# A two-layer encoder on one core: lead-in of the first sublayer with raw x transposed, the norm's division behind the products, and weight jobs that serve both token blocks

## The chip, the cores and the metric

One core of one Trainium2 chip. The metric is device microseconds (us) of the whole program, the median of several runs.

## What is computed

Six sublayers in a row over x of 256 tokens by 1024 channels, float32. The change touches the first one only, a half-step feed-forward network:

```python
def _rmsnorm(x, g, eps=RMS_EPS):
    y = xf * lax.rsqrt(jnp.mean(xf * xf, axis=-1, keepdims=True) + eps)
    return y * g

def _half_ffn(x, g_pre, g_post, w_gate, w_up, w_down):      # widths 1024 -> 2816 -> 1024
    h = _rmsnorm(x, g_pre)
    f = (jax.nn.silu(h @ w_gate) * (h @ w_up)) @ w_down
    return x + 0.5 * _rmsnorm(f, g_post)
```

The six are: this network (a), a convolution module (b), the network twice more with other weights (c, d), differential attention (e), the network again (f).

## The kernel before

**Numbers.** Each product of float32 values is made of three products in a rounded format (`mm3`, L151): both operands are split into a high part (`xTh`, `wh`, cast by ScalarE) and a low part (`xTl`, `wl`, the difference, by VectorE), and high by high, high by low and low by high are added up in PSUM.

**Weight stream.** All weights come in jobs of half a megabyte. `issue` (L107) asks SyncE's queue for the transfer into one of 5 `raw` buffers, casts the high part on ScalarE (L113) and subtracts on VectorE (L114). The subtraction ends the use of the `raw` buffer. `pump` (L119) keeps up to 12 split jobs ahead of the oldest one in use. For sublayer a the jobs are: 0 and 1 the gate columns of chunk 0 (256 columns, 4 tiles of 128 rows each), 2 and 3 its up columns, 4 to 7 the same of chunk 1, 8 to 11 of chunk 2, then six jobs of the down weight, and so on.

**Lead-in.** SyncE asks for the first 128 tokens of x, the norm weights copied to all 128 partitions (`gain`, L174, half a megabyte), jobs 0 and 1, and the other 128 tokens. `prenorm` (L181) squares a token block on ScalarE (L186), multiplies it by the norm weights on VectorE (L188), takes the root on GpSimd (L163) and multiplies by it (L192); `turn` (L201) transposes the result on TensorE (L205) and splits it into `xTh` (L208) and `xTl` (L209).

**Sublayer a.** `ffn` (L317) takes its first two chunks with `proj_x` (L244): a token block is the stationary operand, and one bank of PSUM (`pxa`, 2 banks in turn, pool `ps_gu`) receives gate and up columns side by side, 48 products for each token block and chunk, in the order block 0, block 1 of chunk 0, then of chunk 1. ScalarE applies Silu to the gate half (L330), VectorE multiplies (L332), TensorE transposes the two halves (`hta`, L334). The other chunks go through `projs` (L261): the weight is the stationary operand, each bank (`gua`) takes 48 products, ScalarE applies Silu (L342), VectorE multiplies (L344). Products with the down weight (`acca`, 512 columns) run in between and after.

**Order.** Each engine runs its instructions in a fixed order. The framework's planner chooses that order before the run by the order in the program, by priority, and by when it expects operands; `keep_in_program_order` pins an instruction behind all earlier ones of its engine.

Of the kernel before, what the change touches and what calls it, by code (L numbers as in the profile page):

```python
# [14 lines left out]
ALU = mybir.AluOpType  # L15
# [22 lines left out]
WARM = (16, 6, 6)  # L38

# [10 lines left out]
def trunk_kernel(  # L50
# [56 lines left out]
    def issue(i):  # L107
        src, shape = jobs[i]
        raw = rawp.tile([P, *shape], F32, tag="raw", name=f"raw{i}")
        nc.sync.dma_start(raw, src)  # L110
        hi = wp.tile([P, *shape], F32R, tag="wh", name=f"wh{i}")
        lo = wp.tile([P, *shape], F32R, tag="wl", name=f"wl{i}")
        A.copy(hi, raw)  # L113
        V.tensor_tensor(lo, raw, r32(hi), ALU.subtract)  # L114
        ready[i] = (hi, lo)

    issued, oldest, gone = [0], [0], set()

    def pump():  # L119
        while issued[0] < min(oldest[0] + NW, len(jobs)):  # L120
            issue(issued[0])
            issued[0] += 1
# [11 lines left out]
    class Weight:  # L134
        """Some k tiles of a weight, in jobs of half a megabyte; w(k) gives hi and lo of tile k."""
# [30 lines left out]
    def spread(ms, rows, name):  # L166
        """rows[i] = ms[:, i]^-1/2, the same in every partition."""
# [13 lines left out]
    def prenorm(tb, g, name):  # L181
# [11 lines left out]
        pending.append(lambda: turn(tb, xn, name))  # L193

# [33 lines left out]
    def spin(n, name):  # L228
        """n products that nobody reads: an idle tensor engine drops to half its clock."""
# [4 lines left out]
    def proj(w1, w2, f, name):  # L234
        """[w1 tile f | w2 tile f].T @ xT -> one bank [128, 2*S]."""
# [8 lines left out]
    def proj_x(pairs, order, name):  # L244
        """x[tb] @ [w1 | w2] for pairs of weights i, as (tb, i, bank [128 tokens, 2*FC])."""
# [14 lines left out]

    def projs(pairs, name):  # L261
        """(tile number, bank) of each pair of columns."""
# [12 lines left out]
    class Down:  # L275
        """y[tok, D] += s[:, tok].T @ W over k tiles; the tail one token block after the other."""
# [38 lines left out]
    TURN = [(tb, i) for i in range(2) for tb in range(NTB)]  # L315

    def ffn(hp, jb, name):  # L317
# [10 lines left out]
        for tb, i, ps in proj_x([r[:2] for r in jb[:2]], TURN if name == "a" else TWO, name):  # L328
            sg = sp.tile([P, FC], F32, tag="sg", name=f"sx{name}{tb}{i}")
            A.activation(sg, ps[:, :FC], AF.Silu)  # L330
            h = sp.tile([P, FC], F32, tag="hf", name=f"hx{name}{tb}{i}")
            V.tensor_tensor(h, ps[:, FC:], sg, ALU.mult)  # L332
            for f in range(2):
                T.transpose(turned[i][:, f, tb, :], h[:, f * P:(f + 1) * P], ident)  # L334
        for i in range(2):
            hi, lo = tiles(i)
            split_to(hi, lo, turned[i])
            put(i, hi, lo)
        for kt, ps in projs([(c, jb[c][:2]) for c in range(2, len(jb))], name):
            c, f = divmod(kt, 2)  # L340
            sg = sp.tile([P, S], F32, tag="sg", name=f"sg{name}{kt}")
            A.activation(sg, ps[:, 0, :], AF.Silu)  # L342
# [447 lines left out]
```

## Time and profile before

| | |
|---|---|
| median of 3 runs | 1060.96 us (1059.96 to 1061.01) |
| span of the profiled execution, first to last instruction | 1059.0 us |
| TensorE busy | 1023.4 us |
| VectorE, ScalarE, GpSimd busy | 659.6, 553.7, 72.4 us |
| moved from HBM | 175.40 MB, 167 GB/s over the span |
| first product of the first sublayer | 11.42 us after the span's start |
| first product with the down weight | 47.52 us after the span's start |

The profiled execution has a span of 1059.0 us; the timed figure is taken around the whole execution and is 2.0 us above it. In the views, PE is TensorE, PEld its loads of stationary operands, DVE VectorE, ACT ScalarE, POOL GpSimd, SPq SyncE's queue; L113 is line 113. A matmul's duration is modelled with its pipeline, so the time from one start to the next, not the printed duration, is what it costs in a stream.

### The profile page before, as it was taken

To read this page: it belongs to the slowest core of one execution; us is meant where nothing else is said; L and a number is where in the kernel's file an instruction comes from. 1 tells how busy PE (TensorE), PEld (TensorE's weight loads), DVE (VectorE), ACT (ScalarE), POOL (GpSimd) and SP (SyncE) were. 2 spreads that over 40 slices of the span, in tenths; PEclk is the share of its full clock that TensorE was granted. 3 is DMA by queue.
4 is the path that set the end of the run, shared out by engine and by line. 5 is a ranking of instruction groups with operands and counts; after the bars stand their busy time and mean duration, and the time that the engine had idled before them with its cause. 6 is when DMAs were issued, how large, how long until landed. Compare 5 with 4: busy or idle time off the path is not lost.

```text
span 1059.0 us, 17905 instructions
## 1 busy us (share of the span) xinstructions
PE 1023.4 (97%) x7133; PEld 947.7 (89%) x7133; DVE 659.6 (62%) x1007; ACT 553.7 (52%) x933; POOL 72.4 (7%) x110
## 2 busy tenths in 40 slices
PE   6999999999969999999999999999999999999997
PEld 5899999899967989999989999998899789999995
DVE  6655556679996755455575555566777685555542
ACT  6564445476845644444455445454577665445431
POOL 1000000031560100000010000001000110000000
PEclk9999999999998999999999999999999999999999
DMA  9877465376000666475555665554842255665511
GB/s 296 283 208 221 150 205 179 112 259 197 14 1 0 215 203 218 148 229 177 165 175 185 195 218 151 190 188 133 276 150 91 80 165 180 196 216 155 187 58 40
DMA packets 130492, 177.62 MB, mean 168 GB/s; under 512 B 6173, under 2 KB 112709, under 8 KB 130408
## 3 DMA queue, kind: packets, MB, share of 16 engines
q1 hardware_dynamic: 130408, 176.47, 52.1%
q8 instruction: 56, 0.92, 0.3%
q14 instruction: 28, 0.23, 0.1%
HBM read 175.40 MB, written 1.05 MB: 167 GB/s over the span
## 4 chain that ended last, share of the span: by engine, by line
PE 79%; DVE 10%; issue 3%; ACT 2%; DMA 2%; POOL 2%; SPq 0%; DVEq 0%; POOLq 0%; ACTq 0%
DVE co L474 4%; PE gud L152 3%; PE gua L152 3%; PE gua L154 3%; PE gud L154 3%; PE gud L153 3%; PE gua L153 3%; PE guc L152 3%; PE guf L152 3%; PE guf L154 3%; PE guc L154 3%; PE guc L153 3%; PE guf L153 3%; DVE wl L114 2%; PE accf L152 2%
## 5 line engine op out<-in xcount | busy, mean ns | idle before, releaser
L114 DVE TENSOR_TENSOR wl<-raw,wh 128x1024 fp32r<-128x1024 f32 x320 | 389.7, 1224 | 135.6 <-ACT wh L113 132.8
L113 ACT CAST wh<-raw 128x1024 fp32r<-128x1024 f32 x320 | 333.9, 1051 | 137.0 <-PE accd L154 14.0
L152 PE MATMUL guc<-xTh,wh 128*128 128x256 f32 x288 | 82.1, 285 | 0.0
L152 PE MATMUL guf<-xTh,wh 128*128 128x256 f32 x288 | 82.0, 285 | 0.0
L152 PE MATMUL gud<-xTh,wh 128*128 128x256 f32 x288 | 82.0, 285 | 0.0
L152 PE MATMUL gua<-xTh,wh 128*128 128x256 f32 x288 | 82.0, 285 | 0.0
L154 PE MATMUL guc<-xTh,wl 128*128 128x256 f32 x288 | 81.7, 284 | 0.0
L154 PE MATMUL gua<-xTh,wl 128*128 128x256 f32 x288 | 81.7, 284 | 0.0
L154 PE MATMUL guf<-xTh,wl 128*128 128x256 f32 x288 | 81.7, 284 | 0.0
L154 PE MATMUL gud<-xTh,wl 128*128 128x256 f32 x288 | 81.7, 284 | 0.0
L153 PE MATMUL gua<-xTl,wh 128*128 128x256 f32 x288 | 81.0, 281 | 0.0
L153 PE MATMUL guc<-xTl,wh 128*128 128x256 f32 x288 | 81.0, 281 | 0.0
L153 PE MATMUL guf<-xTl,wh 128*128 128x256 f32 x288 | 80.9, 281 | 0.0
L153 PE MATMUL gud<-xTl,wh 128*128 128x256 f32 x288 | 80.9, 281 | 0.0
L474 DVE SCALAR_TENSOR_TENSOR co<-u,wdw,co 128x256 f32<-128x256 f32 x120 | 61.9, 581 | 0.0
L153 PEld LDWEIGHTS guc<-xTl,wh 128*128 128x128 f32 x288 | 54.7, 190 | 0.5
L153 PEld LDWEIGHTS gua<-xTl,wh 128*128 128x128 f32 x288 | 54.6, 190 | 0.5
L153 PEld LDWEIGHTS guf<-xTl,wh 128*128 128x128 f32 x288 | 54.6, 190 | 0.5
L153 PEld LDWEIGHTS gud<-xTl,wh 128*128 128x128 f32 x288 | 54.6, 190 | 0.5
L152 PEld LDWEIGHTS guc<-xTh,wh 128*128 128x128 f32 x288 | 54.4, 189 | 0.5
L152 PEld LDWEIGHTS gud<-xTh,wh 128*128 128x128 f32 x288 | 54.4, 189 | 0.5
L152 PEld LDWEIGHTS guf<-xTh,wh 128*128 128x128 f32 x288 | 54.4, 189 | 0.5
(357 smaller groups left out, 2672.4 us busy)
## 6 DMA issues: line engine op xcount, KB each, us to landing
raw<-in_ffn_w_gate_dram SPq DMA_DIRECT2D x88, 512.0 KB, 5.1
raw<-in_ffn_w_up_dram SPq DMA_DIRECT2D x88, 512.0 KB, 4.9
raw<-in_ffn_w_down_dram SPq DMA_DIRECT2D x88, 512.0 KB, 4.8
raw<-in_conv_w_pw_dram SPq DMA_DIRECT2D x24, 512.0 KB, 4.5
raw<-in_attn_w_qkv_dram SPq DMA_DIRECT2D x24, 512.0 KB, 4.7
raw<-in_attn_w_o_dram SPq DMA_DIRECT2D x8, 512.0 KB, 4.9
gpre<-in_ffn_norm_pre_dram SPq DMA_DIRECT2D x3, 512.0 KB
x<-in_x_dram SPq DMA_DIRECT2D x2, 512.0 KB
```

The lines of the kernel that those rows point to most:

```text
L113: A.copy(hi, raw)
L114: V.tensor_tensor(lo, raw, r32(hi), ALU.subtract)
L152: T.matmul(o, sh, mh, start=first, stop=False)
L153: T.matmul(o, sh, ml, start=False, stop=False)
L154: T.matmul(o, sl, mh, start=False, stop=last)
L474: tap[ct, t] = V.scalar_tensor_tensor(c, u[:, t:t + S], wdw[:, ct, t:t + 1], c, ALU.mult, ALU.add)
```

## The change

- The first norm is replaced by `first_norm`, with its order on TensorE, ScalarE, VectorE and SyncE pinned by hand. TensorE first multiplies the identity by itself 7 times. The norm weights come as 8 rows of 128 (4 KB) and are transposed into a column per tile (`gc`). Raw x is transposed; VectorE multiplies the transposed tile by its column of norm weights (`scaled`); the high part is cast and the low part subtracted as before (`high`, `low`). Another 3 products of the identity stand between the two token blocks. The squares and the root (`rs`, both blocks in one GpSimd operation) come later, between the splits of jobs 0 to 3. Jobs 4 to 7 are loaded and split in pinned order after them.
- x of block 1 is asked for after job 0 instead of after job 1.
- `proj_jobs` replaces `proj_x` in sublayer a: both token blocks of a chunk have a bank at once, and each job serves first block 0 and then block 1 (12 products each) before the next job is taken.
- The norm's root is applied behind the products: in the first two chunks as the scale of Silu and the scalar of the multiplication; in the nine others as a row copied to all partitions (`row`, made by two transposes and a copy), by two more VectorE multiplications for each of 18 tiles.
- The transposes of chunk 0's result wait until the first job of chunk 1 has served both blocks.

```diff
+WARM0 = (7, 3)
...
     ready = {}
 
-    def issue(i):
+    issued, oldest, gone = [0], [0], set()
+
+    def fetch():
+        i = issued[0]
+        issued[0] += 1
         src, shape = jobs[i]
         raw = rawp.tile([P, *shape], F32, tag="raw", name=f"raw{i}")
-        nc.sync.dma_start(raw, src)
+        return i, raw, nc.sync.dma_start(raw, src)
+
+    def split(i, raw):
+        shape = jobs[i][1]
         hi = wp.tile([P, *shape], F32R, tag="wh", name=f"wh{i}")
         lo = wp.tile([P, *shape], F32R, tag="wl", name=f"wl{i}")
-        A.copy(hi, raw)
-        V.tensor_tensor(lo, raw, r32(hi), ALU.subtract)
         ready[i] = (hi, lo)
-
-    issued, oldest, gone = [0], [0], set()
+        return A.copy(hi, raw), V.tensor_tensor(lo, raw, r32(hi), ALU.subtract)
 
     def pump():
         while issued[0] < min(oldest[0] + NW, len(jobs)):
-            issue(issued[0])
-            issued[0] += 1
+            split(*fetch()[:2])
 
...
+    def first_norm(row):
+        pin = tc.keep_in_program_order
+        ps = ps_gu.tile([P, 2, S], F32, tag="gu", name="warm0")
+        for _ in range(WARM0[0]):
+            pin(T.matmul(ps[:, 0, 0:P], ident, ident, start=True, stop=True))
+        gr = sp.tile([KD, P], F32, tag="gr", name="gr", bufs=1)
+        pin(nc.sync.dma_start(xs[0], x[0, 0:P, :]))
+        pin(nc.sync.dma_start(gr, row.rearrange("(k p) -> k p", p=P)))
+        w = []
+        def load():
+            i, raw, d = fetch()
+            pin(d)
+            w.append((i, raw))
+        load()
+        pin(nc.sync.dma_start(xs[1], x[0, P:S, :]))
+        for _ in range(3):
+            load()
+        pg = ps_acc.tile([P, 512], F32, tag="acc", name="pg")
+        pin(T.transpose(pg[:, 0:KD], gr, ident[:KD, :KD]))
+        gc = sp.tile([P, KD], F32, tag="gc", name="gc", bufs=1)
+        pin(V.tensor_copy(gc, pg[:, 0:KD]))
+        parts = sp.tile([P, 2, 2], F32, tag="parts0", name="parts0", bufs=1)
+        pts, y = {}, {}
+        def turned(tb, pool, tag):
+            for j in range(2):
+                pt = pts[tb, j] = pool.tile([P, 4, P], F32, tag=tag, name=f"pta{tb}{j}")
+                for q in range(4):
+                    k = 4 * j + q
+                    pin(T.transpose(pt[:, q, :], xs[tb][:, k * P:(k + 1) * P], ident))
+        def at(t, tb, j):
+            return t[:, 4 * j:4 * j + 4, tb * P:(tb + 1) * P]
+        def scaled(tb, j):
+            y[tb, j] = sp.tile([P, 4, P], F32, tag="xn", name=f"ya{tb}{j}", bufs=3)
+            pin(V.tensor_tensor(y[tb, j], pts[tb, j], gc[:, 4 * j:4 * j + 4].unsqueeze(2).to_broadcast([P, 4, P]),
+                                ALU.mult))
+        def high(tb, j):
+            pin(A.copy(at(xTh, tb, j), y[tb, j]))
+        def low(tb, j):
+            pin(V.tensor_tensor(at(xTl, tb, j), y[tb, j], r32(at(xTh, tb, j)), ALU.subtract))
+        def square(tb, j):
+            junk = sp.tile([P, 512], BF16, tag="junk", name=f"ja{tb}{j}", bufs=1)
+            pin(A.activation(junk, xs[tb][:, HALF[j]], AF.Square, scale=1.0 / 32, accum_out=parts[:, tb, j:j + 1]))
+        def both(n):
+            for ins in split(*w[n]):
+                pin(ins)
+        turned(0, ps_acc, "acc")
+        for _ in range(WARM0[1]):
+            pin(T.matmul(ps[:, 1, 0:P], ident, ident, start=True, stop=True))
+        turned(1, ps_mi, "mi")
+        scaled(0, 0)
+        scaled(0, 1)
+        both(0)
+        high(0, 0)
+        low(0, 0)
+        high(0, 1)
+        scaled(1, 0)
+        square(0, 0)
+        high(1, 0)
+        low(1, 0)
+        low(0, 1)
+        both(1)
+        scaled(1, 1)
+        high(1, 1)
+        low(1, 1)
+        both(2)
+        square(0, 1)
+        both(3)
+        square(1, 0)
+        square(1, 1)
+        ms = sp.tile([P, 2], F32, tag="ms0", name="ms0", bufs=1)
+        pin(V.scalar_tensor_tensor(ms, parts[:, :, 0], RMS_EPS, parts[:, :, 1], ALU.add, ALU.add))
+        rs = sp.tile([P, 2], F32, tag="rs0", name="rs0", bufs=1)
+        G.tensor_tensor(rs, ms, nhalf, ALU.pow)
+        for n in range(4, 8):
+            load()
+            both(n)
+        return rs
...
+    def proj_jobs(pairs, name):
+        pin = tc.keep_in_program_order
+        for i, pair in enumerate(pairs):
+            banks = [ps_gu.tile([P, 2 * FC], F32, tag="gu", name=f"px{name}{tb}{i}") for tb in range(NTB)]
+            for m, w in enumerate(pair):
+                for k0 in range(0, KD, w.per):
+                    for tb, ps in enumerate(banks):
+                        c = slice(tb * P, (tb + 1) * P)
+                        for n, (s, v) in enumerate(((xTh, 0), (xTh, 1), (xTl, 0))):
+                            for k in range(k0, k0 + w.per):
+                                pin(T.matmul(ps[:, m * FC:(m + 1) * FC], s[:, k, c], w(k)[v],
+                                             start=n + k == 0, stop=n == 2 and k == KD - 1))
+                        if (m, k0) == (0, 0):
+                            if tb:
+                                hook()
+                w.free()
+            for tb, ps in enumerate(banks):
+                yield tb, i, ps
...
-    TURN = [(tb, i) for i in range(2) for tb in range(NTB)]
-
-    def ffn(hp, jb, name):
+
+    def ffn(hp, jb, name, late=None):
...
         turned = [ps_mi.tile([P, 2, NTB, P], F32, tag="mi", name=f"ht{name}{i}") for i in range(2)]
-        for tb, i, ps in proj_x([r[:2] for r in jb[:2]], TURN if name == "a" else TWO, name):
+        lead = [r[:2] for r in jb[:2]]
+        rs, row = late, None
+        for tb, i, ps in proj_x(lead, TWO, name) if late is None else proj_jobs(lead, name):
             sg = sp.tile([P, FC], F32, tag="sg", name=f"sx{name}{tb}{i}")
-            A.activation(sg, ps[:, :FC], AF.Silu)
             h = sp.tile([P, FC], F32, tag="hf", name=f"hx{name}{tb}{i}")
-            V.tensor_tensor(h, ps[:, FC:], sg, ALU.mult)
-            for f in range(2):
-                T.transpose(turned[i][:, f, tb, :], h[:, f * P:(f + 1) * P], ident)
+            if late is None:
+                A.activation(sg, ps[:, :FC], AF.Silu)
+                V.tensor_tensor(h, ps[:, FC:], sg, ALU.mult)
+            else:
+                A.activation(sg, ps[:, :FC], AF.Silu, scale=rs[:, tb:tb + 1])
+                V.scalar_tensor_tensor(h, ps[:, FC:], rs[:, tb:tb + 1], sg, ALU.mult, ALU.mult)
+
+            def flip(tb=tb, i=i, h=h):
+                for f in range(2):
+                    T.transpose(turned[i][:, f, tb, :], h[:, f * P:(f + 1) * P], ident)
+
+            if late is not None and i == 0:
+                pending.append(flip)
+            else:
+                flip()
         for i in range(2):
             hi, lo = tiles(i)
             split_to(hi, lo, turned[i])
             put(i, hi, lo)
+        if rs is not None:
+            pr = ps_mi.tile([P, S], F32, tag="mi", name=f"pr{name}")
+            for tb in range(NTB):
+                T.transpose(pr[:, tb * P:(tb + 1) * P], rs[:, tb:tb + 1].to_broadcast([P, P]), ident)
+            row = hp.tile([P, S], F32, name="row", bufs=1)
+            A.copy(row, pr)
         for kt, ps in projs([(c, jb[c][:2]) for c in range(2, len(jb))], name):
             c, f = divmod(kt, 2)
             sg = sp.tile([P, S], F32, tag="sg", name=f"sg{name}{kt}")
-            A.activation(sg, ps[:, 0, :], AF.Silu)
+            if row is None:
+                A.activation(sg, ps[:, 0, :], AF.Silu)
+            else:
+                V.tensor_tensor(sg, ps[:, 0, :], row, ALU.mult)
+                A.activation(sg, sg, AF.Silu)
+                V.tensor_tensor(sg, sg, row, ALU.mult)
             h = sp.tile([P, S], F32, tag="hf", name=f"hf{name}{kt}")
             V.tensor_tensor(h, ps[:, 1, :], sg, ALU.mult)
...
-        ("a", lambda p: ffn(p, J00, "a"), ffn_norm_pre[0, 0], ffn_norm_post[0, 0], True, conv_params),
+        ("a", lambda p: ffn(p, J00, "a", late), ffn_norm_pre[0, 0], ffn_norm_post[0, 0], True, conv_params),
...
-    nc.sync.dma_start(xs[0], x[0, 0:P, :])
-    g = gain(subs[0][2], "prea")
-    for n in range(2):
-        issue(issued[0])
-        issued[0] += 1
-    nc.sync.dma_start(xs[1], x[0, P:S, :])
     with tc.high_priority():
-        prenorm(0, g, "a")
-        hook()
-    prenorm(1, g, "a")
+        late = first_norm(subs[0][2])
     for n, (name, body, _, post, half, also) in enumerate(subs):
```

## Rows read from the trace of the kernel before

**Rows 1.** The page, part 1: busy time of each engine.
```profile
PE 1023.4 (97%) x7133; PEld 947.7 (89%) x7133; DVE 659.6 (62%) x1007; ACT 553.7 (52%) x933; POOL 72.4 (7%) x110
```
**Rows 2.** Waits of TensorE, whole run: who for whom, us in total, times, longest.
```profile
PE pta L205 <- DVE xna L192: 8.7, 1, 8.7
PE pv L557 <- DVE sum L552: 6.3, 1, 6.3
```
**Rows 3.** Windows: length, busy us (instructions) by engine, granted clock, DMA share, GB/s.
```profile
8.66:17.02 8.36, 6.98 (x29) 6.29 (x30) 7.23 (x11) 7.02 (x11) 1.46 (x1) 1.00 1.09 357
17.02:47.52 30.50, 28.53 (x237) 27.95 (x237) 24.05 (x26) 19.97 (x24) 0.00 (x0) 1.00 0.90 303
```
**Rows 4.** Timeline, all engines, to 12.8 us: start, length, instruction, [idle before <- releaser].
```profile
4.54 0.63 ACT L186 ACTIVATE ja<-x 128x512 bf16<-128x512 f32 x1 [2.14 <-DMA x<-in_x_dram]
...
6.92 1.29 DVE L188 TENSOR_TENSOR xna<-x,gprea 128x512 f32<-128x512 f32 x2 [0.66 <-DMA gprea<-in_ffn_norm_pre_dram]
...
8.66 1.97 PE L205 MATMUL pta<-ident,xna 128*128 128x128 f32 x8 [8.66 <-DVE xna L192]
...
12.80 0.58 PE L154 MATMUL pxa<-wh,xTl 128*128 128x256 f32 x1 [0.58 <-DVE xTl L209]
```
**Rows 5.** Timeline of TensorE and ScalarE, 15 to 18.2 us: one product's spacing, casts.
```profile
15.10 0.41 PE L152 MATMUL pxa<-wh,xTh 128*128 128x256 f32 x1
15.32 0.41 PE L153 MATMUL pxa<-wl,xTh 128*128 128x256 f32 x1
...
15.65 1.05 ACT L113 CAST wh<-raw 128x1024 fp32r<-128x1024 f32 x1 [0.46 <-DMA raw<-in_ffn_w_gate_dram]
...
17.16 1.05 ACT L113 CAST wh<-raw 128x1024 fp32r<-128x1024 f32 x1 [0.46 <-DMA raw<-in_ffn_w_gate_dram]
...
18.06 0.28 PE L154 MATMUL pxa<-wh,xTl 128*128 128x256 f32 x1
...
18.18 0.28 PE L152 MATMUL pxa<-wh,xTh 128*128 128x256 f32 x1
```
**Rows 6.** Timeline, 22 to 47.6 us: Silu, the multiplications behind it, a pause, the first down product.
```profile
22.00 1.28 ACT L330 ACT_TABLE_LOAD   x1
...
23.30 0.38 ACT L330 ACTIVATE sxa<-pxa 128x256 f32<-128x256 f32 x1
23.58 3.88 ACT L113 CAST wh<-raw 128x1024 fp32r<-128x1024 f32 x4
24.65 2.36 DVE L114 TENSOR_TENSOR wl<-raw,wh 128x1024 fp32r<-128x1024 f32 x2 [1.60 <-ACT wh L113]
...
26.93 0.42 DVE L332 TENSOR_TENSOR hxa<-pxa,sxa 128x256 f32<-128x256 f32 x1
...
27.49 0.41 PE L334 MATMUL hta<-ident,hxa 128*128 128x128 f32 x2 [1.38 <-DVE hxa L332]
...
47.52 0.40 PE L152 MATMUL acca<-wh,hha 128*128 128x512 f32 x1
```
**Rows 7.** Groups by line, 0 to 47.7 us: busy us, mean ns of one.
```profile
L186 ACT ACTIVATE ja<-x 128x512 bf16<-128x512 f32 x4 | 2.5, 633 | 2.2 <-DMA x<-in_x_dram 2.1
L208 ACT CAST xTh<-pta 128x512 fp32r<-128x512 f32 x4 | 2.3, 583 | 1.7 <-PE pta L205 1.7
L209 DVE TENSOR_TENSOR xTl<-pta,xTh 128x512 fp32r<-128x512 f32 x4 | 2.6, 683 | 0.0
L163 POOL TENSOR_TENSOR rspa<-mspa,nhalf 128x1 f32<-128x1 f32 x2 | 2.0, 1012 | 12.6 <-DVE mspa L161 12.6
```
**Rows 8.** The tile `raw`, 0 to 30 us: from issue to landing.
```profile
DMA to landing us min/median/max: 4.1/6.2/7.6
```
**Rows 9.** Windows of the convolution's end, columns as in rows 3.
```profile
312.00:316.00 4.00, 0.00 (x0) 0.00 (x0) 3.77 (x10) 0.42 (x1) 4.00 (x2) 0.77 0.00 0
316.00:320.00 4.00, 1.98 (x9) 2.01 (x10) 2.32 (x7) 0.83 (x2) 0.25 (x1) 0.50 0.01 2
```
**Rows 10.** Window of the rest of sublayer a, columns as in rows 3.
```profile
50.00:190.00 140.00, 140.00 (x1004) 131.78 (x1003) 76.50 (x93) 70.16 (x91) 0.00 (x0) 1.00 0.61 192
```
## The prediction

> **What bounds the kernel now.** I read the busy shares first, then TensorE's waits, then the windows that hold them. TensorE is busy 1023.4 of 1059.0 us [rows 1]: what it doesn't do early, it does late. Of its waits over the whole run, the one before the first transposes (8.7 us) is the longest, and the convolution's end (6.3) is untouched by this change [rows 2]. So the change is worth what it shortens up to the first product with the down weight, at 47.52 us [rows 6]. From 50 to 190 us TensorE is busy all the time [rows 10], and later stages follow from it: an earlier start should arrive at the end undiminished.
>
> Three losses lie before 47.52. The first transposes wait until 8.66, because x lands at 4.54, the copied norm weights only at 6.92, and the root and two multiplications follow [rows 4]. Then the same product costs 0.21 us (15.10 to 15.32) and later 0.12 (18.06 to 18.18) [rows 5]: the first is 256 columns at 1.2 GHz, the second near 2.4. The column of the granted clock says 1.00 in both windows [rows 3], so at the start it is the spacing that shows the level. Unbroken products ran from 12.80 to 17.02 before it rose [rows 4, 3]. Third, pauses after 17.02: the window of 30.50 us holds 237 instructions; some 220 products at 0.12 and 16 transposes at about 0.1 are 28.0, so 2.5 us are lost. The largest pause ends at 27.49, when VectorE's multiplication behind the first Silu is done; it had stood behind two weight subtractions [rows 6].
>
> **What must be done by 47.52.** 192 products of the first two chunks and 48 of the third: 240 x 0.12 = 28.8 us, and 8 transposes of the result, 0.9. That work is the same after the change, with two transposes (0.2) added for the row. The question is where it starts and what pauses it has.
>
> **The loads.** The copied norm weights (half a megabyte) leave the queue for 4 KB. Two casts that waited for transfers started 1.51 us apart (15.65, 17.16) [rows 5], so a half megabyte costs 1.5 us there. Job 0 then lands 1.5 us after x, at 6.0, or at the latest when the copied weights did, 6.92; I take 6.3, near the first, because it is the same place in the queue with other rows to read. Block 1 of x follows at 7.8, jobs 1 to 4 at 9.3 to 13.8. The small load is not in the trace; it stands right behind x in the same queue, so it lands between x (4.54) and job 0 (6.3). I take 4.7; the late end costs up to 1 us, since the transposes of block 0 stand behind it on TensorE. The loads of SyncE are only reordered; nothing else was queued there so early.
>
> **TensorE's start.** The ten products of the identity run before x is there or between the two blocks' transposes. Each is at most two streams of 128 columns at the slow level if it is like the other float32 products; even at 0.4 us each the seven end at about 4.4, before x. They cost nothing on the path. Block 0 is transposed from 4.8 to 6.4 (8 took 1.97 us at the slow level [rows 4]), block 1 from 7.8 to 9.3. The first product can run at about 9, not 11.42.
>
> **ScalarE and VectorE set the pace after that.** Both queues are in order. Durations: cast of a job 0.97 in a row (3.88 for 4) [rows 6], subtraction 1.18 (2.36 for 2) [rows 6], cast of half a token block 0.58 and a square 0.63 [rows 7] plus 0.1 to read its sum, subtraction of half a block 0.68 [rows 7]. `scaled` reads PSUM like that last one, so 0.68; its broadcast column is not in the trace, and I take no more. Following the pinned order from 6.3:
> - Job 0 is cast until 7.3 and subtracted until 8.5; block 0's high half is there at 7.9, its low half at 9.2.
> - VectorE reaches `scaled(1,0)` at 9.2, ScalarE's `high(1,0)` waits for it until 9.9, and job 1's cast stands behind that: 10.3 to 11.4. Its subtraction ends at 12.9.
> - `scaled(1,1)` comes after it, until 13.5; `high(1,1)` waited 2.1 us for it and ends at 14.1. Job 2 is split by 16.3, job 3 by 18.0. The squares end at 18.2, the root (0.56 to 1.46 on GpSimd, mean 1.0 [rows 7]) at 19.5.
> - Jobs 4 to 7 follow. Job 7 needs the `raw` buffer that job 2's subtraction frees at 16.3 and at least 4.1 us to land [rows 8]: 20.4, cast until 22.2, subtracted until 24.0.
>
> TensorE meanwhile takes each job for both blocks, 24 products or 2.9 us. It waits at job 0 for block 1 (10.4), at job 1 for its subtraction (12.9) and for `high(1,1)` (14.1), at job 2 for its subtraction (16.3), and has job 3 to itself: chunk 0 ends at 21.7. If it runs at the slow level until 13.5, as from 12.80 to 17.02 before, these waits absorb it and chunk 0 ends at 22.5. So the clock at the start matters less than it seems, and the ten extra products hardly at all.
>
> **The new wait.** Chunk 1 needs both banks of the pool, and chunk 0 holds both until Silu and the multiplication have read them; before, one bank's 48 products hid the other's. Silu waits for the chunk's last product and the root, and in ScalarE's queue it stands behind the casts that are ready earlier, jobs 6 and 7. Then the table is loaded (1.28) and Silu runs (0.38) [rows 6], which I keep although its scale is now a column and was a constant: 22.2 + 1.7 = 23.9. VectorE multiplies behind job 7's subtraction, 24.0 to 24.4. Chunk 1 starts at **24.5**, a pause of 2.8 us that wasn't there. Bounds: with both Silus ahead of job 6, 22.6; with the multiplication behind job 8 or 9, as it stood behind two subtractions before [rows 6], 26.5 to 27.7. I take the middle order, since jobs 0 to 7 are pinned and of high priority and job 8 lands only at 22.1.
>
> The Trainium skill ("ScalarE: Activation LUTs", What ACT_TABLE_LOAD costs) gives about 2.66 us for such a switch, 1.28 of load and 1.38 of draining. The row agrees with the load alone: Silu starts at 23.30, 0.02 after it [rows 6]. By the page's figure chunk 1 would start 1.4 us later and the time would be 1058.3; the measurement decides.
>
> **The sum.** 24.5 + 96 products (11.5) + 8 transposes (0.9) + row (0.2) + 0.2 at the next change of banks (there VectorE has 1.4 us for 0.6 of work, unless a subtraction stands ahead) + 48 products (5.8) = 43.1, against 47.52: 4.4 us earlier.
>
> **The later tiles.** 18 tiles get two more VectorE operations of 256 columns, 0.42 each as the multiplication [rows 6], 15.1 us, where VectorE is busy 76.5 of 140 [rows 10]. TensorE has 5.8 us of other products while a tile goes through its chain, which grows by about 1 us. That cover hides it; without it, each tile would cost 1 us. At the last tiles no down products stand in between and I allow 0.3. Down-weight jobs are no limit: from 50 to 190 us the DMA engines are busy 0.61 [rows 10].
>
> So the span falls by 4.1, from 1059.0 to 1054.9; the median of the runs lies 2.0 above the span, and I forecast **1056.9 us**, with 1055.0 to 1060.1 for the orders named above.
>
> **Rivals.**
> - *The clock falls in the pause.* TensorE stood still from 312 to 316 and the granted clock fell to 0.50, the 1.2 GHz level [rows 9]; after the pause that ended at 27.49 no slow product is to be seen, and it was half as long as mine. If it falls, 4.2 us of products run at 0.21 instead of 0.12 and lose 1.8: 1058.7. The Trainium skill ("TensorE: Matmul & The Clock Gate", A second HAM failure mode: psum-queue depth-cycling) warns of this very pattern, idling between groups as banks are cycled. Chance 0.14.
> - *The first Silu comes far behind the weight splits: slower.* Jobs 8 to 11 are in the program before Silu. Each one ahead of it costs about 1.2 us, as `raw` buffers come free: behind job 9 chunk 1 starts at 27.8, behind job 10 at 29.2, behind job 11 at 30.4. From job 10 on the gain is gone, and so long a pause also brings the clock down (1.8): 1056.9 + 5.9 + 1.8 = **1064.6**. For it speaks the pause of before, against it that Silu is ready at 21.9 and job 10 lands only at 26. Chance 0.07.
> - *The start does not carry to the end:* the pinned early orders give the gain, but VectorE's added work or another order later takes it back: 1060.9. TensorE's full window [rows 10] speaks against it. Chance 0.06.
>
> **How the numbers follow.** Forecast 0.73. A measurement of this kernel tells 0.2% or 2.1 us from no change, so faster means below 1058.8; of the forecast 0.10 lies above that, where the multiplication stands behind job 8 or 9. The clock rival lies at the edge: 0.06 faster, 0.08 the same. Faster 0.63 + 0.06 = 0.69; same 0.10 + 0.08 + 0.06 = 0.24; slower 0.07. The range from 1053.5 (Silu early and the small load early) to 1060.3 (late bank and clock) should hold the time 8 times in 10.
>
> **What would show it.** Job 0's cast at about 6.3 and the first product near 9; TensorE's waits in the first 17 us named by the splits of block 1 and jobs 1 and 2; a wait of chunk 1's first product on VectorE's multiplication, ended near 24.5; the first down product near 43.1; the window after it of unchanged length. Wrong would be a start after 10, a pause beyond 5 us, 0.21 us between products after 24.5, or new waits between 50 and 190 us.

## The result and the profile after

The changed kernel takes **1066.34 us** (median of 5 runs, 1065.64 to 1066.62) against 1059.96 (5 runs, 1059.07 to 1061.01) for the kernel before: a ratio of 1.0055, 95% interval 1.0043 to 1.0066. The forecast was 1056.9 and a gain; it is a loss, of 5.8 us by the ratio. The profiled execution's span is 1064.8 us.

Waits of TensorE in the first 60 us of the kernel after (who for whom, us in total, times, longest):

```profile
PE pxa L366 <- DVE hxa L451: 9.0, 1, 9.0
PE warm L205 <- POOL ones_e L93: 1.6, 1, 1.6
PE pta L232 <- DMA x<-in_x_dram: 1.5, 1, 1.5
```

The 8.7 us before the first transposes [rows 2] are gone. In their place stands one wait that is longer: a product of the lead-in (L366) waits 9.0 us for VectorE's multiplication behind the Silu (L451). It is the wait that the prediction named and put at 2.8 us. Who was late is read from the timeline of ScalarE (start, length, instruction, [idle before <- releaser]):

```profile
8.19 1.04 ACT L122 CAST wh<-raw 128x1024 fp32r<-128x1024 f32 x1 [5.79 <-DMA raw<-in_ffn_w_gate_dram]
...
21.55 1.05 ACT L122 CAST wh<-raw 128x1024 fp32r<-128x1024 f32 x1 [0.66 <-DMA raw<-in_ffn_w_gate_dram]
24.26 1.04 ACT L122 CAST wh<-raw 128x1024 fp32r<-128x1024 f32 x1 [1.66 <-DMA raw<-in_ffn_w_up_dram]
27.88 1.04 ACT L122 CAST wh<-raw 128x1024 fp32r<-128x1024 f32 x1 [2.58 <-DMA raw<-in_ffn_w_up_dram]
29.40 1.04 ACT L122 CAST wh<-raw 128x1024 fp32r<-128x1024 f32 x1 [0.47 <-DMA raw<-in_ffn_w_gate_dram]
30.46 1.28 ACT L450 ACT_TABLE_LOAD   x1
31.75 0.84 ACT L450 ACTIVATE sxa<-pxa,rs 128x256 f32<-128x256 f32 x2
```

The first row is job 0, the next four are jobs 5 to 8. Each of these waits for its transfer, job 7 for 2.58 us; it has landed and is cast at 27.88, where the forecast had it landed at 20.4 and cast until 22.2, and job 8 is cast ahead of the Silu besides. Why the transfers are late stands in SyncE's queue:

```profile
4.94 2.55 SPq L115 DMA_DIRECT2D raw<-in_ffn_w_gate_dram  x1
7.54 0.89 SPq L536 DMA_DIRECT2D wdw_r<-in_conv_w_dw_dram  x1
8.47 1.24 SPq L537 DMA_DIRECT2D par_r<-in_conv_b_pw_dram  x1
9.75 0.32 SPq L538 DMA_DIRECT2D par_r<-in_conv_b_dw_dram  x1
10.53 0.38 SPq L115 DMA_DIRECT2D raw<-in_ffn_w_gate_dram  x1
11.05 0.30 SPq L539 DMA_DIRECT2D par_r<-in_conv_ln_g_dram  x1
12.55 0.28 SPq L540 DMA_DIRECT2D par_r<-in_conv_ln_b_dram  x1
14.04 0.36 SPq L180 DMA_DIRECT2D gposta<-in_ffn_norm_post_dram  x1
15.54 0.39 SPq L115 DMA_DIRECT2D raw<-in_ffn_w_up_dram  x1
20.20 0.34 SPq L180 DMA_DIRECT2D gpre<-in_mix_norm_pre_dram  x1
20.58 0.43 SPq L740 DMA_DIRECT2D la<-in_attn_lambda_q_dram  x1
21.11 0.38 SPq L115 DMA_DIRECT2D raw<-in_ffn_w_up_dram  x1
```

Between jobs 4 and 7 (the four `raw` rows) stand eight loads that are needed much later: the convolution's five, two gains of half a megabyte each (for the end of this sublayer and for a later norm), the first of attention's. The kernel before asks for the convolution's first parameter only at 45.18 us:

```profile
45.18 0.40 SPq L399 DMA_DIRECT2D wdw_r<-in_conv_w_dw_dram  x1
```

The diff doesn't touch these lines; their place is the planner's, and it moved (why, no run shows). Job 7 is issued behind the second gain and the attention load, and that gain had itself waited. SyncE's waits up to 50 us in the kernel after have it:

```profile
SPq L115 <- DVE wl L122: 14.9, 12, 2.7
SPq L180 <- DMA wdw_r<-in_conv_w_dw_dram: 4.3, 1, 4.3
```

The DMA engines were not short of time meanwhile (last but one column: their busy share):

```profile
18.00:20.20 2.20, 2.15 (x18) 1.95 (x17) 1.67 (x3) 2.17 (x6) 0.00 (x0) 1.00 0.47 157
20.20:21.50 1.30, 1.30 (x13) 1.30 (x12) 0.57 (x1) 0.70 (x1) 0.71 (x1) 1.00 0.24 79
```

What was late is one part of a load. In this trace a weight job tells its landing in 16 parts: 15 of job 5's had come by 16.90 and the last only at 21.53, 15 of job 6's by 19.64 and the last at 24.24. `wdw_r`, of 124 KB, told the end of its landing at 20.18, 12.6 us after its issue. That one of the 16 DMA engines was behind with `wdw_r` would explain both, but is not shown.

The windows show what the pause then does to the clock (columns as in rows 3):

```profile
22.70:32.80 10.10, 1.12 (x10) 0.92 (x9) 5.32 (x5) 5.46 (x7) 0.00 (x0) 0.77 0.89 289
32.80:39.16 6.36, 6.36 (x32) 6.36 (x33) 5.53 (x8) 6.26 (x8) 0.00 (x0) 0.56 0.89 284
39.16:46.00 6.84, 6.84 (x59) 6.84 (x58) 5.69 (x6) 4.32 (x5) 0.00 (x0) 1.00 0.99 336
```

Behind the pause TensorE is busy all the time, but does 32 instructions in 6.36 us and then 59 in 6.84: the granted clock was 0.56, near the 1.2 GHz level, and came back to 1.00.

**Where the loss arises.** I counted the products of sublayer a (without the transposes) that had started by a given time, each at its cost in a full-speed stream (0.119 us for 256 columns, 0.234 for 512). Work done, in us:

| by | before | after |
|---|---|---|
| 20 us | 5.0 | 7.9 |
| 30 us | 12.4 | 11.4 |
| 50 us | 31.1 | 25.1 |
| 100 us | 81.0 | 74.7 |
| 180 us | 160.6 | 154.3 |

The earlier start is real: 2.9 us ahead at 20 us. By 50 us the changed kernel is 6.0 us behind, by 180 it is 6.3. The span is 5.8 us longer, so the loss is made before 50 us. The first product with the down weight doesn't tell this: it runs at 47.32 us, against 47.52. But before the change the 48 products of the third chunk had run ahead of it, and now they run behind it; at 0.12 us each they are 5.8 us.

### The profile page after: what moved, and what is told of

It is laid out like the page before. It is cut to its first block, busy times and chain, and to the rows that moved or that the text cites. A ratio compares the mean times of both kernels' runs of the same rounds, so it can differ in the third digit from the quotient of the medians.

```text
span 1064.8 us, 17966 instructions
## 1 busy us (share of the span) xinstructions
PE 1029.2 (97%) x7156; PEld 953.0 (89%) x7156; DVE 671.4 (63%) x1039; ACT 555.1 (52%) x934; POOL 71.3 (7%) x109
## 4 chain that ended last, share of the span: by engine, by line
PE 79%; DVE 9%; DMA 4%; issue 3%; ACT 2%; POOL 2%; SPq 0%; DVEq 0%; POOLq 0%; ACTq 0%
DVE co L611 4%; DMA raw<-in_ffn_w_gate_dram 3%; PE guc L158 3%; PE gua L158 3%; PE guc L157 3%; PE gua L157 3%; PE gua L156 3%; PE guc L156 3%; PE gud L158 3%; PE guf L158 3%; PE gud L157 3%; PE guf L157 3%; PE guf L156 3%; PE gud L156 3%; DVE wl L122 2%
## 5 line engine op out<-in xcount | busy, mean ns | idle before, releaser
L156 PEld LDWEIGHTS gua<-xTh,wh 128*128 128x128 f32 x288 | 54.7, 190 | 0.5
```

The lines of the kernel that those rows point to most:

```text
L156: T.matmul(o, sh, mh, start=first, stop=False)
```

## The experiments

There are four suspects in one chain: the loads between the weight jobs, the order on ScalarE (job 8 ahead of the Silu), the two banks that chunk 1 waits for, and the clock. Three edits take the first three away, one at a time and together. In the table, "next" is the start of the next sublayer's first transposes (203.79 us in the kernel before, 210.04 after); the ratio is to runs of the kernel before on the same chip. Each edit has one trace, and in the twelve traces below the cast of job 0 begins between 6.05 and 8.19 us, with the loads held or not; so where the loads are held, "next" can differ by up to 2 us without any edit.

| what differs from the changed kernel | next | median, us | ratio, 95% interval |
|---|---|---|---|
| nothing | 210.04 | 1066.34 | 1.0055, 1.0043 to 1.0066 |
| loads behind every job traced so far | 205.85 | 1062.88 | 1.0034, 1.0020 to 1.0048 |
| loads behind job 20 | 204.52 | 1062.94 | 1.0033, 1.0021 to 1.0045 |
| order | 208.02 | 1064.13 | 1.0042, 1.0029 to 1.0056 |
| banks | 203.84 | 1060.40 | 1.0003, 0.9992 to 1.0014 |
| loads behind every job, order | 204.39 | 1058.43 | 0.9990, 0.9980 to 1.0000 |
| loads behind job 20, order | 202.10 | 1058.17 | 0.9980, 0.9970 to 0.9990 |
| loads behind job 20, banks | 199.43 | **1054.67** | 0.9947, 0.9928 to 0.9966 |
| loads behind job 20, order, banks | 197.78 | 1055.36 | 0.9960, 0.9948 to 0.9972 |
| loads behind job 20, older product order | 204.77 | 1063.20 | 1.0023, 1.0011 to 1.0035 |
| products in the pause | 212.40 | 1068.51 | 1.0078, 1.0064 to 1.0092 |
| no row multiplications | 209.26 | 1065.36 | 1.0055, 1.0041 to 1.0069 |

**The loads, behind every job traced so far.** `lastd[0]` holds the newest weight job's load.

```diff
-        return i, raw, nc.sync.dma_start(raw, src)
+        lastd[0] = nc.sync.dma_start(raw, src)
+        return i, raw, lastd[0]
...
-        nc.sync.dma_start(t, row.partition_broadcast(P))
+        with after(lastd[0]):
+            nc.sync.dma_start(t, row.partition_broadcast(P))
...
+        with after(lastd[0]):
             nc.sync.dma_start(wdw_r, conv_w_dw[0])
```

(and so for the other parameters.)

> Edit to the changed kernel: the loads of the convolution's and attention's parameters and of the later norms' weights are queued behind the weight jobs that precede them in the program, instead of standing between jobs 4 and 9. Theory A (these loads hold up jobs 6 to 9 in SyncE's queue and on the DMA engines, and ScalarE's in-order queue holds Silu behind those jobs): job 6 lands by 17.5 and job 7 by 21 us instead of 24.3 and 27.9; Silu and its multiplication still stand behind jobs 8 and 9, so chunk 1 starts near 27.5 instead of 32.8; about 5 us less than the changed kernel, 1060 to 1062 us. Theory B (it is the order Silu behind the splits alone, and the extra loads only fill a queue that waits for raw buffers anyway): chunk 1 starts within 1 us of 32.8, time within 1.5 us of 1066.3.

By the ratios 2.2 us of the loss are back, less than the first theory asks (1062.88, not 1060 to 1062). Jobs 4 to 7 now land early and are cast without a gap, but that is not the whole of it:

```profile
19.09 3.88 ACT L123 CAST wh<-raw 128x1024 fp32r<-128x1024 f32 x4
24.12 1.04 ACT L123 CAST wh<-raw 128x1024 fp32r<-128x1024 f32 x1 [1.15 <-DMA raw<-in_ffn_w_gate_dram]
25.18 1.28 ACT L452 ACT_TABLE_LOAD   x1
26.48 0.84 ACT L452 ACTIVATE sxa<-pxa,rs 128x256 f32<-128x256 f32 x2
```

With every load out of the way ScalarE still waits 1.15 us for job 8 and casts it, with the Silu behind it. TensorE's wait is still 7.0 us, and chunk 1 starts at 30.05, not at 27.5.

**Loads and order.** Job 8 and those behind it enter the program only after chunk 0's Silus.

```diff
+    cap = [8]
...
-        while issued[0] < min(oldest[0] + NW, len(jobs)):
+        while issued[0] < min(oldest[0] + NW, len(jobs), cap[0]):
...
             if late is not None and i == 0:
+                if tb:
+                    cap[0] = len(jobs)
                 pending.append(flip)
```

> Edit on top of the held loads: jobs 8 and later are traced only after chunk 0's Silu, so that Silu and its multiplication stand right behind job 7, as the forecast assumed. Theory A: Silu ends near 24, chunk 1 starts near 24.5, the first down product near 43, time 1056 to 1058.5, faster than the kernel before. Theory B (the gain is lost elsewhere, as in the later tiles' longer chain on VectorE): TensorE starts chunk 1 early all the same but the time stays above 1060.

This is the chain as the prediction wrote it: Silu at 24.16 (forecast 23.9), chunk 1 at 25.21 (24.5) after a wait of 2.3 us (2.8). The time is within the measurement of the kernel before all the same. TensorE is 2.2 us of work ahead of it at 180 us (162.8 against 160.6) and 0.7 behind at 190 (169.0 against 169.7): the parameters, held too long, are issued only at 172.19, TensorE waits 1.1 us for `wdw_r`, and from 186 to 188 us the granted clock is 0.50.

```profile
172.19 0.35 SPq L543 DMA_DIRECT2D wdw_r<-in_conv_w_dw_dram  x1
```

```profile
PE pp L554 <- DMA wdw_r<-in_conv_w_dw_dram: 1.1, 1, 1.1
186.00:188.00 2.00, 2.00 (x6) 1.55 (x5) 0.62 (x2) 0.17 (x1) 0.00 (x0) 0.50 1.04 352
```

So this way of holding the loads has a cost of its own, and the other runs that hold them queue them behind job 20 instead (here against the first edit):

```diff
-        lastd[0] = nc.sync.dma_start(raw, src)
+        d = nc.sync.dma_start(raw, src)
+        if i <= 20:
+            lastd[0] = d
```

**Loads alone, behind job 20.**

> The changed kernel with the later sublayers' parameters and gains queued behind weight job 20 (a few jobs after the lead's own, as the kernel before had them) and nothing else changed. Theory A (the loads between the weight jobs held job 7 back, and the convolution's parameters came too late in the run that queued them behind every job traced): casts of jobs 4 to 7 near 19 us again, the longest wait of TensorE 7 us, no wait for the parameters near 180 us, and 0.6 to 2 us less than that run's 1062.9: 1061 to 1062.3. Theory B (it is not the place of the loads that made that run slow at 180 us): 1062.9 again.

```profile
PE pxa L370 <- DVE hxa L455: 6.7, 1, 6.7
```

The wait for the parameters near 180 us is gone, yet the time is 1062.94, that of the first run with the loads held: the first theory's 0.6 us or more did not come. At 190 us this run is 1.0 us of work behind the kernel before (168.7 against 169.7); the rest of its 3.5 us arises later, in part in sublayers that the edit doesn't touch (the profiled execution is 0.7 us behind at the next sublayer's transposes and 1.6 at the end). Where and why stays open.

**Order alone**, the loads left where the planner put them:

> The changed kernel with the order alone: job 8 and those behind it enter the program after chunk 0's Silus, while the later sublayers' loads stay between the weight jobs as in the changed kernel. Theory A (the loads are the larger cause): jobs 6 and 7 still land near 25 and 27.9 us, the Silu comes at 29.5 to 30.5 us in place of 31.75, chunk 1 at 30.3 to 31.3, and the time falls by 1.5 to 3 us: 1063.3 to 1065. Theory B (the Silu's place behind job 8 is the larger cause): chunk 1 starts near 25 us and the time falls by 6 us or more, to 1060 or less.

It went by the first theory: job 7 is still cast only at 28.08, the Silu runs at 30.43, chunk 1 starts at 31.48, and by the ratios 1.4 us are gained.

**Order with loads behind job 20.**

> The same, and job 8 and those behind it enter the program only after chunk 0's two Silus, so that ScalarE does the Silus right behind job 7's cast. Theory A (two causes, the loads between the jobs and the place of the first Silus): Silu near 24.2 us, TensorE's wait for the banks 2.3 us, first down product near 38.7 us, and the lead of 2.8 us that this order had over the kernel before until 180 us is kept to the end: 1055.5 to 1057. Theory B (an earlier start is lost later anyway, because weights set the pace): 1058.4 or more, as in the run with the parameters late.

The chunk's timeline in this run:

```profile
26.02 1.17 PE L372 MATMUL pxa<-wh,xTh 128*128 128x256 f32 x4 [2.35 <-DVE hxa L457]
26.99 1.05 PE L372 MATMUL pxa<-wl,xTh 128*128 128x256 f32 x4
27.85 1.05 PE L372 MATMUL pxa<-wh,xTl 128*128 128x256 f32 x4
28.70 1.01 PE L372 MATMUL pxa<-wh,xTh 128*128 128x256 f32 x4
29.54 0.63 PE L372 MATMUL pxa<-wl,xTh 128*128 128x256 f32 x4
```

1058.17 us, 2.1 below the kernel before, and its lead of work is kept past 190 us (1.5 us at 180, 1.6 at 190; the 2.8 us that the first theory names are 2.2 by this count). It is 1.2 us short of what the first theory asks. Chunk 1 starts at 26.02 here (ScalarE began jobs 4 to 7 at 19.73 in this run), and behind a pause of only 2.35 us four products take 0.86 us (26.99 to 27.85), not 0.47. From 26.02 to 29.54 sixteen products cost 3.52 us in place of 1.9: 1.6 us for the clock. That is the prediction's first rival (1.8 us, 1058.7), and this run gives nearly its time.

**Banks.** Chunk 1 takes its two banks from the accumulators' pool. Two things go with it: the hook for chunk 0's flips (the transposes of its result) moves to the second weight, and `Down` is made after the lead-in.

```diff
-            banks = [ps_gu.tile([P, 2 * FC], F32, tag="gu", name=f"px{name}{tb}{i}") for tb in range(NTB)]
+            pool, tag = ((ps_gu, "gu"), (ps_acc, "acc"))[i]
+            banks = [pool.tile([P, 2 * FC], F32, tag=tag, name=f"px{name}{tb}{i}") for tb in range(NTB)]
```

This edit alone, loads and order as in the changed kernel:

> The changed kernel with one edit: chunk 1's two banks are taken from the accumulators' four, so that chunk 1's products wait for no Silu; the later sublayers' loads stay between the weight jobs, and the first Silus stay behind job 8's cast. Theory A (the loads cost their time only through the bank: the Silus wait behind them, and the products wait for the Silus): chunk 1's products start at 23 us and then follow the casts of jobs 4 to 7, which end near 21, 22.6, 25.3 and 29, so that chunk 1 ends near 32 to 33 us in place of 46, and the time falls by 5 to 9 us, to 1057.5 to 1061.5. Theory B (the loads take the transfers' time, so that the weights behind chunk 1 are late as well): chunk 1 ends near 33 us, but the first tile products and down products then wait for weights, and the time falls by 3 us or less, to 1063 or more.

```profile
PE hta L456 <- DVE hxa L452: 3.5, 3, 2.0
```

```profile
32.74 0.44 PE L456 MATMUL hta<-ident,hxa 128*128 128x128 f32 x2 [0.94 <-DVE hxa L452]
35.17 0.44 PE L456 MATMUL hta<-ident,hxa 128*128 128x128 f32 x2 [1.99 <-DVE hxa L452]
...
36.40 1.05 PE L367 MATMUL pxa<-wh,xTl 128*128 128x256 f32 x4
```

The largest gain of a single edit, 5.5 us by the ratios, though job 7 is still cast at 27.82 and the Silu still runs at 31.69. Chunk 1 follows chunk 0 without a gap, and 72 of its 96 products are done by 31.6. There the flips of chunk 0's result stand in TensorE's order and wait for the Silus, 0.94 and 1.99 us (the third wait, 0.60, is a flip of chunk 1). The last 24 products run from 35.36 to 39.7, most of them 0.21 us apart, so chunk 1 ends some 7 us later than the first theory has it. So the late loads still cost time here.

With the loads behind job 20 as well, the Silus still behind job 8:

> The changed kernel with the later loads behind job 20 and chunk 1's banks from the accumulators; the first Silus stay behind job 8's cast, since all jobs enter the program as in the changed kernel. Theory A (the Silus' place costs only because the bank waits for them): within 1 us of the run that had the order mended too, 1054.4 to 1056.4. Theory B (the order costs by itself, through the half-done tile or the flips): 1057.5 or more.

```profile
22.70:32.80 10.10, 10.10 (x88) 10.07 (x87) 7.73 (x9) 7.91 (x10) 0.00 (x0) 1.00 0.91 319
```

**1054.67 us**, 5.6 below the kernel before by the ratio and the lowest of all. On top of the banks, holding the loads is worth 5.9 us by the ratios; without the banks it was 2.3. In the window in which the changed kernel did 10 products and transposes, this one does 88, at full clock. The time lies where the first theory has it. With the order mended too:

> The same again, and chunk 1's two banks are taken from the accumulators' four, so that chunk 1 waits for no Silu. Theory A (the new wait for chunk 0's banks is the third cost): TensorE goes from chunk 0 to chunk 1 without the 2.3 us wait, its first product of chunk 1 at 22.5 to 23.5 us, and the time 1 to 3 us below the run that has the order alone: 1053 to 1055.5. Theory B (chunk 1 is then paced by the weight casts or by the accumulators that chunk 1 holds): first product of chunk 1 earlier, but the first down product no earlier than 38.5 us and the time within 0.5 us of that run.

TensorE is busy for all of 20 to 30 us, and the time is as the first theory has it, 1055.36. (The first down product, at 41.50, is later than the 39.46 of the run with the order alone, but tile products now run ahead of it: by 40 us 27.1 us of work are done, there 23.6.) The intervals of this run and the one before it overlap, so no worth of the order can be told once the banks are free. Job 0 and jobs 4 to 7 in this run:

```profile
6.44 1.04 ACT L125 CAST wh<-raw 128x1024 fp32r<-128x1024 f32 x1 [4.04 <-DMA raw<-in_ffn_w_gate_dram]
...
18.12 3.88 ACT L125 CAST wh<-raw 128x1024 fp32r<-128x1024 f32 x4
```

**The older product order**, with the loads behind job 20: a token block passes all four jobs of a chunk before the other does.

```diff
-        for tb, i, ps in proj_x(lead, TWO, name) if late is None else proj_jobs(lead, name):
+        for tb, i, ps in proj_x(lead, TWO, name) if late is None else proj_x(lead, [(tb, i) for i in range(2) for tb in range(NTB)], name):
```

> The changed kernel with the later loads behind job 20 and the lead-in's products in the older order: a token block passes all four jobs of a chunk before the other block does, and the second chunk's bank for a block waits for that block's own Silu. To be set against the run with the loads behind job 20 alone (1062.9). Theory A (weight jobs that serve both blocks save the time that one block waits for weights to land): block 0 follows the casts until 18.5 us, block 1 ends near 24.3, the Silu of block 0 comes behind job 8's cast near 26 us as before, chunk 1 starts near 27 in both, and the time is the same or up to 2 us longer: 1062.5 to 1065. Theory B (holding two banks through a chunk is what brought the wait): the time is 2 us or more shorter, 1061 or less.

1063.20 against 1062.94: no difference that can be told. By 30 us they have done 12.0 and 11.5 us of work. Block 0's first product runs at 8.01 (nothing waits for block 1), but the chain through job 8 and the Silu ends in a 6.6 us wait as well, there in front of the flips. So jobs that serve both blocks neither brought the loss nor, in this setting, a gain. Whether they gain with the banks free wasn't tried.

**The clock in the pause.** 40 products of 512 columns that nobody reads, between chunk 0 and chunk 1:

```diff
+            if i:
+                keep = ps_acc.tile([P, 512], F32, tag="acc", name="keep")
+                for _ in range(40):
+                    pin(T.matmul(keep, xTh[:, 0, 0:P], xTh[:, 0:2, :], start=True, stop=True))
```

> Edit to the changed kernel: 40 products of 512 columns that nobody reads stand between chunk 0 and chunk 1 on TensorE, 8.7 us at the full clock, to fill the pause. Theory A (part of the loss is the clock, which fell in the pause): chunk 1 starts at about the same time, its products are 0.12 us apart from the first on, about 2 us less than the changed kernel, 1064.3. Theory B (the clock costs nothing because chunk 1 waits for other things): within 0.5 us of 1066.3 or slower.

```profile
32.36 0.75 PE L370 MATMUL pxa<-wh,xTh 128*128 128x256 f32 x4 [0.31 <-DVE hxa L455]
32.94 0.64 PE L370 MATMUL pxa<-wl,xTh 128*128 128x256 f32 x4
...
49.33 0.44 PE L459 MATMUL hta<-ident,hxa 128*128 128x128 f32 x2 [2.66 <-DVE hxa L455]
...
50.30 0.41 PE L157 MATMUL gua<-xTl,wh 128*128 128x256 f32 x1
50.51 0.41 PE L158 MATMUL gua<-xTh,wl 128*128 128x256 f32 x1
```

The clock stays at 1.00 through chunk 1, which ends 2 us earlier, but the time is 2.2 us longer than the changed kernel's, and the first theory's 1064.3 did not come. ScalarE reaches chunk 1's Silu only at 48.29 (47.42 in the changed kernel), so its flips now wait 2.66 us, and soon behind that wait the products run 0.21 us apart: the slow stretch is moved, not spared. By 60 us 32.5 us of work are done, against 34.9 in the changed kernel. So this run does not price the clock by itself; the spacing behind the pauses does.

**The later tiles.** Without the two added VectorE multiplications in the 18 tiles behind the lead-in; this leaves the root's scaling out of those tiles.

> Edit to the changed kernel: the two added VectorE multiplications of each of the 18 later tiles are left out (the norm's root is then missing from these tiles). Theory A (TensorE's other products cover them, as predicted): within 0.6 us of the changed kernel's 1066.3. Theory B (the longer chain holds up the down products or the end of the sublayer): 2 us or more less.

1065.36 us, the same ratio as the changed kernel: these operations cost nothing that the runs can tell. The trace shows one thing more. Its loads stand as in the changed kernel, but job 0 (first row) came early, and job 7 (last row) is late all the same:

```profile
6.33 1.05 ACT L122 CAST wh<-raw 128x1024 fp32r<-128x1024 f32 x1 [3.93 <-DMA raw<-in_ffn_w_gate_dram]
...
27.60 1.04 ACT L122 CAST wh<-raw 128x1024 fp32r<-128x1024 f32 x1 [2.43 <-DMA raw<-in_ffn_w_up_dram]
```

## Why the prediction was wrong, point by point

- **"The loads of SyncE are only reordered; nothing else was queued there so early."** This step failed. It was true of the trace of before and was carried over to the kernel after, where eight other loads stand between jobs 4 and 7. Job 7 lands at 27.88, 7.5 us later than the 20.4 of the forecast. In this trace 2.0 of it is the pace before it (job 2's subtraction frees the buffer at 18.3, not 16.3), 2.8 the queue (issued at 21.11), and 2.7 the flight (6.8 us from issue to the cast, where 4.1 was taken, the shortest of [rows 8]). But the pace is not what made it late: in the run without the row multiplications, whose loads stand as in the changed kernel, job 0 is cast at 6.33 and the buffer is free at 16.51, as forecast, and job 7 is still cast only at 27.60. In the run with the loads behind job 20, order and banks mended, job 0 is cast at 6.44 and job 7 at 20.95, the last of the four in a row from 18.12.
- **"I take the middle order, since ... job 8 lands only at 22.1."** This failed too, and the loads were not its cause. With them held back, ScalarE's queue had job 8 ahead of the Silu, waited for its landing (cast at 24.12 and 23.81), and VectorE's multiplication stood behind job 9's subtraction: chunk 1 started at 30.05 and 29.74, beyond the bound of 27.7. The argument was that a Silu that is ready first goes first, but the queue is in order and its order is set before the run. In the changed kernel the two steps add up to 24.5 + 6.7 (job 7's cast ends at 28.9 instead of 22.2) + 1.6 (job 8) = 32.8, where chunk 1 starts.
- **The new wait** was named rightly: its place, its releaser, and what it hangs on. With both premises mended it is 2.3 us (2.8 forecast). Its price was judged by its length alone; the banks edit shows that the wait as such is the larger cost, since without it even the late loads leave the kernel level with the one before.
- **The clock** was a rival at 0.14 and turned out to belong in the forecast: every pause of 2.3 us or more behind chunk 0 was followed by products at 0.21 us. The length alone doesn't decide it: behind the 1.38 us of the kernel before [rows 6] there were none, but the granted clock fell behind the wait of 1.1 us for `wdw_r` that the run with the loads behind every job and the order mended has near 183 us (0.50 from 186 to 188). In the changed kernel the first 24 products of chunk 1 go from 32.80 to 38.09, 5.3 us in place of 2.9. The Trainium skill ("TensorE: Matmul & The Clock Gate", A second HAM failure mode: psum-queue depth-cycling) describes frequent short idling between groups of products as banks are cycled, with the clock falling and rising again. Here it is one pause, of 2.3 to 10.5 us, at one change of banks, and the fall behind it agrees (granted clock 0.56 from 32.80 to 39.16).
- **The slower rival** (1064.6) had the right shape: a first Silu far behind the splits, then the clock. Its cause, jobs 8 to 11, was only partly the right one (in the changed kernel job 8 alone stands ahead of the first Silu), and its 0.07 too little. That its time lies so near 1066.34 is in part luck, since it leaves out the late loads.
- **The start.** Job 0 is cast at 8.19, not 6.3, and block 1 is transposed at 9.59, not 7.8. The first product runs at 10.44, not 9. Block 0 of x was there as forecast (its transposes start at 5.05, forecast 4.8), but job 0 came 3.1 us behind that and not 1.5. Chunk 0 ends at 23.7 (21.7 forecast). This step is not refuted by it: over the twelve traces job 0 is cast between 6.05 and 8.19, and where it is cast at 6.33 chunk 0 ends at 21.9. The profiled execution of the changed kernel has the latest start of all, and the loss doesn't hang on it: from the early start chunk 1 starts at 32.51, from the late one at 32.80. In spite of the late start the gain at 20 us is 2.9 us.
- **The table load** is 1.28 us and the Silu starts 0.01 after it (30.46, 31.75); by the Trainium skill's figure in "ScalarE: Activation LUTs" (What ACT_TABLE_LOAD costs), 2.66 us a switch, it would start an estimated 1.4 us later. The row holds, as [rows 6] did. What was missed is that the early attention load brings its Exp forward, and with it two more table loads (36.38 and 46.13).
- **The later tiles** are hidden, as forecast: VectorE is busy 80.52 of the 130 us from 50 to 180 (69.66 before), TensorE 130.00 in both, and the run without the operations has the same ratio.
- **"An earlier start should arrive at the end undiminished"** held within about a microsecond in both directions: of the 6.0 us lost by 50 us 5.8 are in the span, and the 4.5 us won by the best version (35.6 us of work at 50 us, against 31.1) are 5.0 in its profiled span (1054.0 against 1059.0) and 5.6 by the ratio of its runs. It did not hold with the loads alone behind job 20: 0.7 us behind at the next sublayer, 3.5 by the ratio, for no known reason.

## What to carry to other kernels

When an edit pins or reorders loads at the start, everything else that may stand in that queue has to be placed again: a trace of before shows where the planner put it then, not where it will put it. A step that makes one engine wait for a result at the end of a chain over three others (load, cast, Silu, multiplication) was best bought off here with a buffer: two banks from a pool that lay idle gave 5.5 us where mending the links one at a time gave 1.4 and 2.3. Such gains don't add up: once the banks were free, the loads were worth 5.9. And a new pause of TensorE is priced with the half-speed products behind it.

## What the runs showed that I had not expected

- A load at the head of SyncE's queue waited 4.3 us for another load to land (`gpre` for `wdw_r`), and job 7 stood behind it. The two are eight loads apart in the queue, and in this trace each of the first loads has one of eight semaphores, in turn: the ninth, `wdw_r`, has that of the first, the seventeenth, `gpre`, that of `wdw_r`. So a small load that lands late can hold back a large one that has nothing to do with it.
- The half-speed stretch behind a pause depends little on the pause: 3.5 us of it behind 2.35 us (order, loads behind job 20), 2.9 behind 6.7 (those loads alone), some 6 behind 9.0 (the changed kernel), 4.8 behind 10.5 (no row multiplications). The start itself varies: in the run with the banks edit alone, the first eight products take 1.86 us (10.52 to 12.38), while in the changed kernel the first four take 0.55 (10.44 to 10.99).
